# First projections of a two-layer kernel: shift and scale from feature-major weights on VectorE, the next k-tile prepared during this one's products

## Chip, cores and metric

The kernel runs on one core of a Trainium2 chip. The metric is device time in microseconds (us) of one execution; lower is better. All inputs are float32 in HBM and the output is float32.

## What is computed

Two layers run one after the other on 256 tokens of width 1024. The change is in the very first step of the first layer: the shift and scale that come from the condition vector `c`, the normalised and modulated input `h`, and the first columns of `h @ w_in`. Cut to what matters:

```
def rmsnorm(x, g):
    xf = x.astype(jnp.float32)
    xf = xf * lax.rsqrt(jnp.mean(xf * xf, axis=-1, keepdims=True) + EPS)
    return xf.astype(x.dtype) * g
...
    c_act = jax.nn.silu(c)
...
    mod = c_act @ ada_w + ada_b
    sh1, sc1, gt1, sh2, sc2, gt2 = [m[:, None, :] for m in jnp.split(mod, 6, axis=-1)]

    h = rmsnorm(x, mix_pre_g) * (1.0 + sc1) + sh1
    proj = h @ w_in
```

After it follow a state-space branch and a short convolution, a feed-forward block, and a second layer with two kinds of attention and another feed-forward block. None of their arithmetic is touched.

## The kernel before

Everything is kept transposed, features on the 128 partitions and the 256 tokens along a row. The width of 1024 is therefore 8 k-tiles. For each k-tile `t` the first stage makes `h(t)`, a 128x256 tile, and multiplies it with 1568 columns of `w_in` (12 blocks of 128 and one of 32), adding up over `t` in six PSUM banks `xbc` and in a part of the bank `dtps`.

Products in float32 precision are made from two reduced-precision parts: an operand is split into a rounded part `hi` (ScalarE, the CAST rows) and a remainder `lo` (VectorE, the TENSOR_TENSOR rows `lo<-raw,hi`). Each block then takes three products: hi by hi, hi by lo and lo by hi (`mm3`), so a k-tile has 39 products. For `h` the parts are called `hh` and `hl` in the rows. The weights come in halves ("units"), for the first stage of 768 and 800 columns, later of 1024. Six buffers `raw` take what the DMA brings, and five pairs of buffers hold `hi` and `lo`. A unit may thus be cast up to five ahead of the products; a new `lo` waits until TensorE has done with the unit five before it.

Shift and scale for k-tile `t` need 256 columns of `ada_w` (128 of each), all 1024 rows of them: `ada0[t]`, two tiles `ada0a` and `ada0b` of 512 KB each, in the order of the loop also 512 KB to a DMA. The rows of `ada_w` lie on partitions, so the sum over them is a sum over partitions. `mod_acc` lets VectorE multiply six of the eight row blocks by `silu(c)` (one column `cact[:, k]` of 128 values per block) and add them up in `ada0acc` (one TENSOR_SCALAR and five SCALAR_TENSOR_TENSOR instructions of 128x256). `mod_sum` lets TensorE multiply the other two blocks by `cact`, and add `ada0acc` by a product with `ones`: six matmuls of one column, each two rows in the trace because their operands are float32. Then VectorE adds the bias (`m<-ps,pf`), `mod_h` makes `hf` and `hh` on ScalarE, and `mod_lo` makes `hl` on VectorE. These matmuls of k-tile `t + 1` stand in TensorE's order in the middle of k-tile `t`, between `half(0)` and `half(1)`.

Ahead of the loop stand the sums of squares of `x` (`sq`, then products with `ones` into `dtps`), the inverse root (VectorE, then a power on GpSimd), its spreading over the partitions by two products with `ident`, the scaling of `x` by it (the first k-tile on VectorE, the other seven on GpSimd), and 20 products of `ones` with `ones` that only keep TensorE active.

The order of this stage is written out by hand on every engine. DMAs go out in program order on one queue, SyncE's; a load of a `raw` buffer waits there until VectorE has made the `lo` from it, and what stands behind it waits too. After the loop a planner takes over: it keeps a model time of every engine and picks the next piece of work from a list of tasks; a task `caster` casts the units ahead, with the highest priority while fewer than five are ready. So what this stage leaves behind (how many units are ready, where each engine stands) moves the planner's order after it.

Later in the same kernel, other parts of `ada_w` are stored with their features on partitions. There one VectorE instruction multiplies a 128x1024 tile by `crow`, which is `silu(c)` on every partition, and sums along the row (`ada_mul`; CUSTOM_DVE_ANT_0 `raw<-raw,crow` in the trace, with a small instruction behind it that reads the sum out).

Of the kernel before, what the change touches and what calls it, by code (L numbers as in the profile page):

```python
# [31 lines left out]
def _plan():  # L32
# [21 lines left out]
    def b_list(w, k0, nk, cols):  # L54
        return lambda i: (i[w][k0 * 128:(k0 + nk) * 128][:, cols].reshape(nk, 128, len(cols))
                          .transpose(1, 0, 2).reshape(128, -1))

    for t in range(8):
        cols = np.concatenate([np.arange(128) + 128 * t, np.arange(128) + 1024 + 128 * t])
        plan.append((("ada0", t), 2048, b_list("ada_w", 0, 8, cols)))  # L60
        c2 = np.concatenate([np.arange(128) + XBC0 + 128 * f for f in XBC_FT0] + [np.arange(32) + DT0])
        plan.append((("w0", t), 1568, b_list("w_in", t, 1, c2)))
    for g in range(4):
# [175 lines left out]
WARM = 20  # L239
SPLIT0, EARLY = 8, 2  # L240
ROT_SPARE = 6
UPORDER = ("0a 0b 1a 0l 1b 1l", "0a 0b 1a 1b 0l 1l")
LAST_C = "gt1"
# [172 lines left out]
def _body(ctx: ExitStack, tc: tile.TileContext, wst, pf_d, rows_d, cst_d, xT_d, x_d, w2_d, out_d):  # L416
# [18 lines left out]
    def P(name, j=0, n=1, parts=128):  # L435
        return pf[:parts, PF[name][0] + j:PF[name][0] + j + n]
# [203 lines left out]
    def ab(src, j):  # L640
        return src[:, j * T:j * T + T]
# [162 lines left out]
    nc.sync.dma_start(cst[:, 128:], cst_d[:, 128:ROT0])  # L804
    ada0_dma(3)
    cact = const.tile([128, 16], F32, name="cact")
    AC.activation(cact, P("c", 0, 16), AF.Silu)
    xbc = [bank() for _ in range(6)]
    dtps, adps = bank(), bank()
    h = HL("h")  # L810
    acc0, m01 = {}, {}
    PK = (0, 2, 2, 2, 2, 2, 2, 2)

    def ws0(t, k):
        return ada0[t][k // 4].rearrange("p (k c) -> p k c", k=4)[:, k % 4]

    def mod_acc(t, k0, k1):

        if t < 8:
            if k0 == 0:  # L820
                acc0[t] = fresh1("ada0acc")
                VE.tensor_scalar(acc0[t], ws0(t, PK[t]), cact[:, PK[t]:PK[t] + 1], None, op0=OP.mult)
            for k in range(max(k0, PK[t] + 1), k1):
                VE.scalar_tensor_tensor(acc0[t], ws0(t, k), cact[:, k:k + 1], acc0[t], op0=OP.mult, op1=OP.add)

    def mod_sum(t):
        a = acc0.pop(t)
        for j in range(2):
            o = adps[:, 2 * t + j:2 * t + j + 1]
            for k in range(PK[t]):  # L830
                PE.matmul(o, ws0(t, k)[:, 128 * j:128 * j + 128], cact[:, k:k + 1], start=k == 0, stop=False)
            PE.matmul(o, a[:, 128 * j:128 * j + 128], ones[:, 0:1], start=PK[t] == 0, stop=True)
        del ada0[t]
        ada0_dma(t + 4)
        m = m01[t] = sm.tile([128, 2], F32, name="m01")
        VE.tensor_add(m, adps[:, 2 * t:2 * t + 2], P("b01", 2 * t, 2))
        VE.scalar_tensor_tensor(m[:, 1:2], m[:, 1:2], 1.0, P("g1", t), op0=OP.add, op1=OP.mult)
# [11 lines left out]
    sq = ep.tile([128, 2048], F32, name="sq", tag="E")  # L849
    def cast0():  # L850
        O.cur = _Task(None, 0.0)
        if st["cast"] < 2 * len(keys):
            cast_next()
        O.cur = None

    for _ in range(WARM):
        PE.matmul(xbc[0][:, :128], ones, ones, start=True, stop=True)
    for q in range(4):
        AC.activation(sq[:, 512 * q:512 * q + 512], xT[:, 512 * q:512 * q + 512], AF.Square)
        for k in (2 * q, 2 * q + 1):  # L860
            for t in range(2):
                PE.matmul(dtps[:, t:t + 1], sq[:, 256 * k + 128 * t:256 * k + 128 * t + 128], ones[:, 0:1], start=k == 0 and t == 0,
                          stop=k == 7, skip_group_check=True)
    r2 = sm.tile([128, 2], F32, name="r2")
    mod_acc(0, 0, SPLIT0)
    rsqrt(r2, dtps[:, :2], D, 1e-6)
    mod_acc(0, SPLIT0, 8)
    for t in range(2):
        PE.matmul(dtps[:, 128 + 128 * t:256 + 128 * t], r2[:, t:t + 1].to_broadcast([128, 128]), ident, start=True, stop=True)
    if EARLY > 0:  # L870
        cast0()
    mod_sum(0)
    rs = fresh1("rs")
    AC.copy(rs, dtps[:, 128:384])
    VE.tensor_mul(xTv[:, 0], xTv[:, 0], dtps[:, 128:384])
    for t in range(1, 8):
        GP.tensor_mul(xTv[:, t], xTv[:, t], rs)
    if EARLY > 1:
        cast0()
    hf = mod_h(0)  # L880
    if EARLY < 1:
        cast0()
    mod_lo(0, hf)
    if EARLY < 2:
        cast0()
    mod_acc(1, 0, 8)
    cast0()
    cast0()
    for t in range(8):
        w = W(t)  # L890

        def half(hf_):
            for f in range(6 * hf_, 6 * hf_ + 6):
                mm3(ab(xbc[f // 2], f % 2), w, f * 128, 128, h.hi(t), h.lo(t), t == 0 and f % 2 == 0, t == 7,
                    skip_group_check=True)
            if hf_:
                mm3(dtps[:32, :T], w, 1536, 32, h.hi(t), h.lo(t), t == 0, t == 7)
            parts.pop((t, hf_))
            st["half"] += 1
            st["ahead"] -= 1  # L900

        mod_acc(t + 2, 0, 4)
        cast0()
# [8 lines left out]
        cast0()  # L912
        half(1)
    free(adps)

    O.spawn(caster(), lambda: -1 if st["ahead"] < PHASE[phase[0]][1] else 2)
# [1539 lines left out]
```

## Time and profile before

| | |
|---|---|
| median of 3 runs | 1071.05 us (1067.59 to 1071.38) |
| the profiled execution | 1072.64 us |
| its span, first to last instruction | 1070.7 us |
| TensorE busy | 1036.2 us, 97% of the span |
| VectorE busy | 849.8 us, 79% |
| ScalarE busy | 628.4 us, 59% |
| GpSimd busy | 45.7 us, 4% |
| mean granted clock of TensorE | 0.982 |

A busy share is an average over the whole span. TensorE is busy nearly all the time, so the places where it stands still, and those where it does work that another engine could do, are what there is to look for. Idle time of another engine costs nothing as long as TensorE does not wait for it.

### The profile page before, as it was taken

What the parts mean: (1) busy time and instruction counts of PE and PEld (TensorE: products, weight loads), DVE (VectorE), ACT (ScalarE), POOL (GpSimd) and SP (SyncE); (2) the same over time, 40 slices, a digit from 0 to 9 for tenths busy, and PEclk for the clock granted to TensorE, in tenths of its full rate; (3) what the DMA queues carried; (4) which work ended last, traced back from release to release, by engine and by line L of the source; (5) the groups of instructions that cost most, each with busy time, mean ns of one, the idle gap of its engine ahead of it and who ended that gap; (6) DMA issues with size and microseconds to landing.
All of it is one profiled execution on the core that took longest, in us unless ns stands there. A gap on an engine that the chain in (4) does not pass through costs nothing.

```text
span 1070.7 us, 18920 instructions
## 1 busy us (share of the span) xinstructions
PE 1036.2 (97%) x7183; PEld 957.1 (89%) x7183; DVE 849.8 (79%) x1566; ACT 628.4 (59%) x1230; POOL 45.7 (4%) x66
## 2 busy tenths in 40 slices
PE   7999999999999999999999889998999789999998
PEld 7999999899999979999987779877998679999986
DVE  5878978977987768998886888896889687878843
ACT  3457569378654366656554466768675346666531
POOL 2000000000000000000000010221100000000000
PEclk8999999999999999999999989998999989999999
DMA  9855577767868947676686588854256725555551
GB/s 356 310 197 170 176 244 242 238 208 242 284 211 305 328 171 227 223 262 222 225 302 201 188 304 281 291 204 139 77 159 231 281 91 195 180 181 183 188 185 40
DMA packets 66187, 234.03 MB, mean 219 GB/s; under 512 B 7568, under 2 KB 8624, under 8 KB 65584
## 3 DMA queue, kind: packets, MB, share of 16 engines
q1 hardware_dynamic: 66096, 232.82, 64.4%
q8 instruction: 56, 0.92, 0.3%
q14 instruction: 35, 0.29, 0.1%
HBM read 230.67 MB, written 2.13 MB: 217 GB/s over the span
## 4 chain that ended last, share of the span: by engine, by line
PE 52%; DVE 5%; ACT 3%; DMA 2%; issue 1%; POOL 0%; ACTq 0%; DVEq 0%; POOLq 0%
PE ps L410 52%; DVE lo L410 2%; DMA raw<-in_wst_dram 1%; ACT hi L410 1%; DMA adp<-in_wst_dram 1%; ACT S L410 1%; DVE S L410 1%; ACT jk L410 0%; DVE raw L410 0%; DVE jk L410 0%; DVE ropet L410 0%; DVE qo L410 0%; DVE Sm L410 0%; DVE tmp L410 0%; ACT tmp L410 0%
## 5 line engine op out<-in xcount | busy, mean ns | idle before, releaser
L410 DVE TENSOR_TENSOR lo<-raw,hi 128x1024 fp32r<-128x1024 f32 (+3 forms) x326 | 388.2, 1197 | 149.0 <-ACT hi L410 147.9
L410 ACT CAST hi<-raw 128x1024 fp32r<-128x1024 f32 (+3 forms) x326 | 332.9, 1031 | 216.2 <-PE ps L410 170.5
L410 PE MATMUL ps<-hh,hi 128*128 128x256 f32 (+1 forms) x520 | 152.8, 294 | 4.1 <-ACT hh L410 4.1
L410 PE MATMUL ps<-hl,hi 128*128 128x256 f32 (+1 forms) x520 | 148.8, 286 | 0.5 <-DVE hl L410 0.4
L410 PE MATMUL ps<-hh,lo 128*128 128x256 f32 (+1 forms) x520 | 148.6, 286 | 0.0
L410 PEld LDWEIGHTS ps<-hh,hi 128*128 128x128 f32 (+1 forms) x520 | 100.4, 193 | 5.9 <-ACT hh L410 4.5
L410 PE MATMUL ps<-h4h,hi 128*128 128x256 f32 x352 | 100.9, 289 | 2.8 <-ACT h4h L410 2.8
L410 PEld LDWEIGHTS ps<-hl,hi 128*128 128x128 f32 (+1 forms) x520 | 100.4, 193 | 2.3 <-issue 1.2
L410 PE MATMUL ps<-h4h,lo 128*128 128x256 f32 x352 | 100.7, 288 | 0.0
L410 PEld LDWEIGHTS ps<-hh,lo 128*128 128x128 f32 (+1 forms) x520 | 100.4, 193 | 0.1
L410 PE MATMUL ps<-h2h,hi 128*128 128x256 f32 x352 | 98.4, 283 | 0.0
L410 PE MATMUL ps<-h2h,lo 128*128 128x256 f32 x352 | 98.3, 283 | 0.0
L410 PE MATMUL ps<-h2l,hi 128*128 128x256 f32 x352 | 94.7, 283 | 0.0
L410 PE MATMUL ps<-h4l,hi 128*128 128x256 f32 x352 | 94.5, 283 | 0.0
L410 DVE CUSTOM_DVE_ANT_0 raw<-raw,crow 128x1024 f32<-128x1024 f32 x64 | 76.9, 1219 | 0.0
L410 DVE SCALAR_TENSOR_TENSOR fc<-ps,pf,fc 128x254 f32<-128x254 f32 (+1 forms) x176 | 72.4, 474 | 0.0
L410 PEld LDWEIGHTS ps<-h4h,hi 128*128 128x128 f32 x352 | 69.6, 198 | 3.0 <-ACT h4h L410 3.0
L410 PEld LDWEIGHTS ps<-h4h,lo 128*128 128x128 f32 x352 | 69.5, 197 | 0.0
L410 PEld LDWEIGHTS ps<-h2h,hi 128*128 128x128 f32 x352 | 67.6, 192 | 0.8 <-ACT h2h L410 0.8
L410 PEld LDWEIGHTS ps<-h2h,lo 128*128 128x128 f32 x352 | 67.6, 192 | 0.0
L410 PEld LDWEIGHTS ps<-h2l,hi 128*128 128x128 f32 x352 | 65.4, 192 | 0.0
L410 PEld LDWEIGHTS ps<-h4l,hi 128*128 128x128 f32 x352 | 65.4, 192 | 0.0
(394 smaller groups left out, 2363.6 us busy)
## 6 DMA issues: line engine op xcount, KB each, us to landing
raw<-in_wst_dram SPq DMA_DIRECT2D x364, 512.0 KB, 4.9
adp<-in_wst_dram SPq DMA_DIRECT2D x16, 512.0 KB, 7.2
ada0a<-in_wst_dram SPq DMA_DIRECT2D x8, 512.0 KB, 8.0
ada0b<-in_wst_dram SPq DMA_DIRECT2D x8, 512.0 KB, 8.7
E<-scr SPq DMA_DIRECT2D x4, 1024.0 KB, 6.8
raw<-in_wst_dram SPq DMA_DIRECT2D x8, 400.0 KB, 7.5
raw<-in_wst_dram SPq DMA_DIRECT2D x8, 384.0 KB, 7.3
brow<-in_rows_dram SPq DMA_DIRECT2D x4, 512.0 KB, 7.9
```

The costliest lines, as they stand in the source:

```text
L410: return f(*a, **k)
```

## The change

The weights for shift and scale are stored with features on partitions (the transpose is made on the host, like all other arrangement of weights). VectorE makes each sum with one 128x1024 instruction (`mod_dot`), two for a k-tile, and TensorE takes no part in it. `crow` is loaded right behind `x`, and its silu is made at the start. The casts of a k-tile's two units, its two sums and its bias (`start_cast`, `mod_dot`, `mod_end`) are put ahead of the products of the k-tile before it, and the remainders (`end_cast`, `mod_lo`) behind them in the program's text; all eight k-tiles of `x` are scaled on VectorE, one in each step (`scale_x`). Ahead of the loop, two of the four squares go to VectorE, the inverse root comes before the sums for shift and scale, `h(0)` is made in a shorter way, and its first six blocks are taken pass by pass, with the `lo` of `h` last. The products that keep TensorE active are in three groups of 12, 5 and 6. The loop ends with two units cast ahead instead of four.

```diff
-        cols = np.concatenate([np.arange(128) + 128 * t, np.arange(128) + 1024 + 128 * t])
-        plan.append((("ada0", t), 2048, b_list("ada_w", 0, 8, cols)))
+        plan.append((("ada0", t), 2048, lambda i, t=t: np.concatenate([i["ada_w"][:, o + 128 * t:o + 128 * t + 128].T for o in (0, 1024)], 1)))
...
+    crow = wk.tile([128, 1024], F32, name="crow", bufs=1)
+    row_load(crow, "c")
     nc.sync.dma_start(cst[:, :128], cst_d[:, :128])
...
-    AC.activation(cact, P("c", 0, 16), AF.Silu)
...
-    def mod_acc(t, k0, k1):
+    def mod_dot(t, j):

         if t < 8:
...
+            w = ada0[t][j]
+            VE.tensor_tensor_reduce(out=w, in0=w, in1=crow, scale=1.0, scalar=0.0, op0=OP.mult, op1=OP.add,
+                                    accum_out=m01[t][:, j:j + 1])
+            if j == 1:
+                del ada0[t]
+                ada0_dma(t + 4)
+
+    def mod_end(t):
+        if t < 8:
+            m = m01[t]
+            VE.tensor_add(m, m, P("b01", 2 * t, 2))
+            VE.scalar_tensor_tensor(m[:, 1:2], m[:, 1:2], 1.0, P("g1", t), op0=OP.add, op1=OP.mult)
+
+    def scale_x(t):
+        if t < 8:
+            VE.tensor_mul(xTv[:, t], xTv[:, t], rs)
...
+    def start_cast():
...
+        AC.copy(h_[:, :b - a], r)
...
+    def end_cast(l_, r, h_):
+        VE.tensor_sub(l_, r, h_.bitcast(F32))
+        refill()
...
+    warm(WARM[0])
     for q in range(4):
-        AC.activation(sq[:, 512 * q:512 * q + 512], xT[:, 512 * q:512 * q + 512], AF.Square)
...
+        if q % 2:
+            VE.tensor_mul(o, i, i)
+        else:
+            AC.activation(o, i, AF.Square)
+    AC.activation(crow, crow, AF.Silu)
+    AC.activation(cact, P("c", 0, 16), AF.Silu)
...
+    warm(WARM[1])
     r2 = sm.tile([128, 2], F32, name="r2")
-    mod_acc(0, 0, SPLIT0)
     rsqrt(r2, dtps[:, :2], D, 1e-6)
-    mod_acc(0, SPLIT0, 8)
+    mod_dot(0, 0)
+    mod_dot(0, 1)
...
-    mod_sum(0)
-    rs = fresh1("rs")
-    AC.copy(rs, dtps[:, 128:384])
-    VE.tensor_mul(xTv[:, 0], xTv[:, 0], dtps[:, 128:384])
-    for t in range(1, 8):
-        GP.tensor_mul(xTv[:, t], xTv[:, t], rs)
...
+    warm(WARM[2])
+    mod_end(0)
+    m0 = m01.pop(0)
+    y0 = fresh1("hf")
+    VE.scalar_tensor_tensor(y0, xTv[:, 0], m0[:, 1:2], rs_ps, op0=OP.mult, op1=OP.mult)
+    cast0()
+    AC.activation(h.hi(0), y0, AF.Identity, bias=m0[:, 0:1])
+    VE.scalar_tensor_tensor(h.lo(0), y0, m0[:, 0:1], h.hi(0).bitcast(F32), op0=OP.add, op1=OP.subtract)
+    rs = fresh1("rs")
+    AC.copy(rs, rs_ps)
     cast0()
-    cast0()
+    scale_x(1)
...
-        mod_acc(t + 2, 0, 4)
-        cast0()
-        mod_acc(t + 2, 4, 6)
+        if t < 7:
...
+            r = [start_cast() for _ in range(2)]
...
+        mod_dot(t + 1, 0)
+        mod_dot(t + 1, 1)
+        mod_end(t + 1)
         half(0)
+        half(1)
         if t < 7:
-            mod_sum(t + 1)
             hf = mod_h(t + 1)
-        mod_acc(t + 2, 6, 8)
-        if t < 7:
+            end_cast(*r[0])
             mod_lo(t + 1, hf)
-        cast0()
-        half(1)
+            end_cast(*r[1])
+        else:
+            cast0()
+            cast0()
+        scale_x(t + 2)
...
-    crow_load("c")
```

What stands in the engines' orders at three places follows; in such a row the output stands left of the arrow, and `ps_87` to `ps_94` are the PSUM banks.

VectorE, one step of the loop before (`m_434` holds shift and scale of one k-tile):

```order
L410 TENSOR_SCALAR ada0acc<-ada0a,cact 128x256
L410 SCALAR_TENSOR_TENSOR ada0acc<-ada0a,cact,ada0acc 128x256
L410 TENSOR_TENSOR lo<-raw,hi 128x768
L410 SCALAR_TENSOR_TENSOR ada0acc<-ada0b,cact,ada0acc 128x256 x2
L410 TENSOR_TENSOR m_434<-ps_94,pf 128x2
L410 SCALAR_TENSOR_TENSOR m_434<-m_434,pf 128x1
L410 SCALAR_TENSOR_TENSOR ada0acc<-ada0b,cact,ada0acc 128x256 x2
L410 TENSOR_TENSOR hl_223<-hf,hh_222 128x256
L410 TENSOR_TENSOR lo<-raw,hi 128x800
```

VectorE, one step of the loop of the change (the ISA rows are the sum along a row and the reading out of it):

```order
L408 ISA ada0a,m_287<-ada0a,crow 128x1024
L408 ISA m_287 128x1
L408 ISA ada0b,m_287<-ada0b,crow 128x1024
L408 ISA m_287 128x1
L408 TENSOR_TENSOR m_287<-m_287,pf 128x2
L408 SCALAR_TENSOR_TENSOR m_287<-m_287,pf 128x1
L408 TENSOR_TENSOR lo<-raw,hi 128x768
L408 TENSOR_TENSOR hl_204<-hf,hh_203 128x256
L408 TENSOR_TENSOR lo<-raw,hi 128x800
L408 TENSOR_TENSOR xT<-xT,rs 128x256
```

Six multiplications of 128x256 give way to two of 128x1024, the scaling of `x` has come in, and the bias no longer reads the PSUM bank `ps_94`.

TensorE, in the middle of a k-tile before: the end of `half(0)`, the matmuls of `mod_sum`, and the first of `half(1)`:

```order
L410 MATMUL ps_89<-hl_223,hi 128x256
L410 MATMUL ps_89<-hh_222,lo 128x256
L410 MATMUL ps_94<-cact,ada0a 128x1 x2
L410 MATMUL ps_94<-ones,ada0acc 128x1
L410 MATMUL ps_94<-cact,ada0a 128x1 x2
L410 MATMUL ps_94<-ones,ada0acc 128x1
L410 MATMUL ps_90<-hh_222,hi 128x256
```

The same place in the change, in its second k-tile:

```order
L408 MATMUL ps_89<-hh_203,hi 128x256
L408 MATMUL ps_89<-hl_204,hi 128x256
L408 MATMUL ps_89<-hh_203,lo 128x256
L408 MATMUL ps_90<-hh_203,hi 128x256
L408 MATMUL ps_90<-hl_204,hi 128x256
```

The six matmuls (twelve rows of the trace) are gone, and nothing stands in their place.

ScalarE, the head of its order before:

```order
L410 ACT_TABLE_LOAD
L410 ACTIVATE cact<-pf 128x16
L410 ACTIVATE sq<-xT 128x512 x4
L410 CAST hi<-raw 128x768
L410 COPY rs<-ps_93 128x256
```

And in the change:

```order
L408 ACT_TABLE_LOAD
L408 ACTIVATE sq<-xT 128x512 x2
L408 ACT_TABLE_LOAD
L408 ACTIVATE crow<-crow 128x1024
L408 ACTIVATE cact<-pf 128x16
L408 CAST hi<-raw 128x768
L408 ACTIVATE hh_203<-hf,m_178 128x256
```

Two squares are gone to VectorE, a second load of a table stands behind the other two, and a silu of 1024 columns has come in ahead of the first cast. Behind the loop, the orders of all engines differ in places over about the first third of the program, and are the same from there on.

## Rows read from the trace of the kernel before

**Rows 1.** Busy time in four stretches (instructions); last: granted clock, DMA share, GB/s.

```profile
20.00:30.00 10.00, 7.81 (x51) 7.23 (x51) 9.13 (x18) 2.72 (x5) 1.73 (x2) 0.84 1.03 407
70.80:200.00 129.20, 129.20 (x967) 123.18 (x967) 110.12 (x174) 88.23 (x140) 0.00 (x0) 1.00 0.65 215
580.00:590.00 10.00, 7.34 (x40) 5.95 (x38) 7.50 (x14) 7.85 (x19) 1.62 (x3) 1.00 0.41 154
```

**Rows 2.** Timeline of TensorE at the start: start, length, what, idle before and releaser.

```profile
7.72 3.63 PE L410 MATMUL ps<-ones,sq 128*128 128x1 f32 x32
13.80 1.22 PE L410 MATMUL ps<-cst,r 128*128 128x128 f32 x4 [2.45 <-POOL r L410]
...
17.71 0.58 PE L410 MATMUL ps<-hh,hi 128*128 128x256 f32 x1 [2.04 <-ACT hh L410]
...
28.83 0.38 PE L410 MATMUL ps<-hh,hi 128*128 128x256 f32 x1 [2.07 <-ACT hh L410]
...
30.42 0.41 PE L410 MATMUL ps<-hh,hi 128*128 128x256 f32 x1
30.63 0.41 PE L410 MATMUL ps<-hl,hi 128*128 128x256 f32 x1
```

**Rows 3.** Timeline of TensorE: first product of the last k-tile, and of the next stage.

```profile
66.78 0.28 PE L410 MATMUL ps<-hh,hi 128*128 128x256 f32 x1
...
71.45 0.40 PE L410 MATMUL ps<-hi,hh 128*128 128x512 f32 x1
```

**Rows 4.** Timeline of VectorE in one steady step of the loop.

```profile
52.38 0.16 DVE L410 TENSOR_TENSOR m<-ps,pf 128x2 f32<-128x2 f32 x1 [0.21 <-PE ps L410]
52.57 0.16 DVE L410 SCALAR_TENSOR_TENSOR m<-m,pf 128x1 f32<-128x1 f32 x1
...
53.84 0.43 DVE L410 TENSOR_TENSOR hl<-hf,hh 128x256 fp32r<-128x256 f32 x1 [0.20 <-ACT hh L410]
54.61 0.99 DVE L410 TENSOR_TENSOR lo<-raw,hi 128x800 fp32r<-128x800 f32 x1 [0.34 <-ACT hi L410]
...
56.30 0.95 DVE L410 TENSOR_TENSOR lo<-raw,hi 128x768 fp32r<-128x768 f32 x1
...
58.38 0.16 DVE L410 TENSOR_TENSOR m<-ps,pf 128x2 f32<-128x2 f32 x1 [0.21 <-PE ps L410]
```

**Rows 5.** Timeline of ScalarE in the same step.

```profile
52.77 0.61 ACT L410 ACTIVATE hf<-xT,m 128x256 f32<-128x256 f32 x1 [3.06 <-DVE m L410]
53.40 0.41 ACT L410 CAST hh<-hf 128x256 fp32r<-128x256 f32 x1
```

**Rows 6.** Timeline of VectorE: two sums along a row with `crow`, one behind the other.

```profile
206.22 1.22 DVE L410 CUSTOM_DVE_ANT_0 raw<-raw,crow 128x1024 f32<-128x1024 f32 x1
...
207.37 1.22 DVE L410 CUSTOM_DVE_ANT_0 raw<-raw,crow 128x1024 f32<-128x1024 f32 x1
...
208.60 1.23 DVE L410 TENSOR_TENSOR lo<-raw,hi 128x1024 fp32r<-128x1024 f32 x1
```

**Rows 7.** Timelines of ScalarE, VectorE and GpSimd ahead of the loop.

```profile
0.73 1.28 ACT L410 ACT_TABLE_LOAD   x1 [0.73 <-PEq L2448]
...
6.75 1.15 ACT L410 ACTIVATE sq<-xT 128x512 f32<-128x512 f32 x2 [0.20 <-DMA xT<-in_xT_dram]
10.58 0.83 ACT L410 CAST hi<-raw 128x768 fp32r<-128x768 f32 x1 [2.68 <-DMA raw<-in_wst_dram]
...
8.25 0.35 DVE L410 TENSOR_SCALAR ada0acc<-ada0a,cact 128x256 f32<-128x256 f32 x1 [8.25 <-DMA ada0a<-in_wst_dram]
...
12.47 1.28 POOL L410 TENSOR_TENSOR r<-r,nhalf 128x2 f32<-128x2 f32 x1 [11.48 <-DVE r L410]
```

**Rows 8.** Timeline of VectorE behind the stage: convolutions of one bank, and the next `lo`.

```profile
74.88 2.41 DVE L410 SCALAR_TENSOR_TENSOR cv<-ps,pf,cv 128x255 f32<-128x255 f32 x6
77.22 1.20 DVE L410 TENSOR_TENSOR lo<-raw,hi 128x1024 fp32r<-128x1024 f32 x1
78.35 2.41 DVE L410 SCALAR_TENSOR_TENSOR cv<-ps,pf,cv 128x255 f32<-128x255 f32 x6
```

More of the change, by code (lines that the diff above doesn't have):

```diff
@@ L238 @@
 MARGIN = 0.0
-WARM = 20
-SPLIT0, EARLY = 8, 2
+WARM = (12, 5, 6)
 ROT_SPARE = 6
@@ L810, in _body @@
     h = HL("h")
[L811 to L815, printed above, removed]
-    def mod_acc(t, k0, k1):
-        if t < 8:
[L820 to L837, printed above, removed]
+    m01 = {}
+    def mod_dot(t, j):
+        if t < 8:
+            if t not in m01:
+                m01[t] = sm.tile([128, 2], F32, name="m01")
+            w = ada0[t][j]
[12 more added lines that the diff above has]
+            VE.tensor_mul(xTv[:, t], xTv[:, t], rs)
     def mod_h(t):
@@ L849, in _body @@
     sq = ep.tile([128, 2048], F32, name="sq", tag="E")
+    def start_cast():
+        u = st["cast"]
+        a, b = span(u)
+        r = raws.pop(u)[:, :b - a]
+        h_, l_ = hlp.tile([128, 1024], F32R, name="hi"), hlp.tile([128, 1024], F32R, name="lo")
+        AC.copy(h_[:, :b - a], r)
+        cast_at[divmod(u, 2)] = 0.0
+        parts[divmod(u, 2)] = (h_, l_)
+        st["ahead"] += 1
+        st["cast"] += 1
+        return l_[:, :b - a], r, h_[:, :b - a]
+    def end_cast(l_, r, h_):
+        VE.tensor_sub(l_, r, h_.bitcast(F32))
+        refill()
     def cast0():
@@ L854, in cast0, with warm @@
         O.cur = None
-    for _ in range(WARM):
-        PE.matmul(xbc[0][:, :128], ones, ones, start=True, stop=True)
+    def warm(n):
+        for _ in range(n):
+            PE.matmul(adps[:, :128], ones, ones, start=True, stop=True)
+    warm(WARM[0])
     for q in range(4):
-        AC.activation(sq[:, 512 * q:512 * q + 512], xT[:, 512 * q:512 * q + 512], AF.Square)
[L860 to L863, printed above, removed]
+        o, i = sq[:, 512 * q:512 * q + 512], xT[:, 512 * q:512 * q + 512]
+        if q % 2:
+            VE.tensor_mul(o, i, i)
+        else:
+            AC.activation(o, i, AF.Square)
@@ L864, in _body @@
+    AC.activation(crow, crow, AF.Silu)
+    AC.activation(cact, P("c", 0, 16), AF.Silu)
+    for k in range(8):
+        for t in range(2):
+            PE.matmul(dtps[:, t:t + 1], sq[:, 256 * k + 128 * t:256 * k + 128 * t + 128], ones[:, 0:1], start=k == 0 and t == 0,
+                      stop=k == 7, skip_group_check=True)
+    warm(WARM[1])
     r2 = sm.tile([128, 2], F32, name="r2")
-    mod_acc(0, 0, SPLIT0)
     rsqrt(r2, dtps[:, :2], D, 1e-6)
-    mod_acc(0, SPLIT0, 8)
+    mod_dot(0, 0)
@@ L868, in _body @@
+    mod_dot(0, 1)
+    rs_ps = dtps[:, 128:384]
     for t in range(2):
-        PE.matmul(dtps[:, 128 + 128 * t:256 + 128 * t], r2[:, t:t + 1].to_broadcast([128, 128]), ident, start=True, stop=True)
-    if EARLY > 0:
-        cast0()
-    mod_sum(0)
-    rs = fresh1("rs")
-    AC.copy(rs, dtps[:, 128:384])
-    VE.tensor_mul(xTv[:, 0], xTv[:, 0], dtps[:, 128:384])
-    for t in range(1, 8):
-        GP.tensor_mul(xTv[:, t], xTv[:, t], rs)
-    if EARLY > 1:
-        cast0()
-    hf = mod_h(0)
@@ L881, in _body @@
-    if EARLY < 1:
-        cast0()
[L883 to L886, printed above, removed]
+        PE.matmul(rs_ps[:, 128 * t:128 * t + 128], r2[:, t:t + 1].to_broadcast([128, 128]), ident, start=True, stop=True)
+    warm(WARM[2])
[6 more added lines that the diff above has]
+    VE.scalar_tensor_tensor(h.lo(0), y0, m0[:, 0:1], h.hi(0).bitcast(F32), op0=OP.add, op1=OP.subtract)
@@ L892, in half @@
         def half(hf_):
-            for f in range(6 * hf_, 6 * hf_ + 6):
+            if t == 0 and hf_ == 0:
+                for p, (u, x) in enumerate(((0, h.hi(0)), (1, h.hi(0)), (0, h.lo(0)))):
+                    for f in range(6):
+                        PE.matmul(ab(xbc[f // 2], f % 2), w.hi(f * 128, 128, u), x, start=p == 0 and f % 2 == 0,
+                                  stop=False, skip_group_check=True)
+            for f in range(6 * hf_, 6 * hf_ + 6) if t or hf_ else ():
                 mm3(ab(xbc[f // 2], f % 2), w, f * 128, 128, h.hi(t), h.lo(t), t == 0 and f % 2 == 0, t == 7,
@@ L900, in half @@
             st["ahead"] -= 1
-        mod_acc(t + 2, 0, 4)
-        cast0()
-        mod_acc(t + 2, 4, 6)
+        if t < 7:
+            O.cur = _Task(None, 0.0)
+            r = [start_cast() for _ in range(2)]
+            O.cur = None
+        mod_dot(t + 1, 0)
+        mod_dot(t + 1, 1)
+        mod_end(t + 1)
         half(0)
+        half(1)
         if t < 7:
-            mod_sum(t + 1)
             hf = mod_h(t + 1)
-        mod_acc(t + 2, 6, 8)
-        if t < 7:
+            end_cast(*r[0])
             mod_lo(t + 1, hf)
-        cast0()
-        half(1)
+            end_cast(*r[1])
[3 more added lines that the diff above has]
+        scale_x(t + 2)
     free(adps)
@@ L929, in _body @@
     ADA2 = ("sha", "sca", "ga", "shf", "scf", "gf")
-    crow = wk.tile([128, 1024], F32, name="crow", bufs=1)
-    crow_is = []
+    crow_is = ["c", True]
     def crow_load(c):
```

1 line of the change is left out of this document (removed).

## The prediction

> **What bounds the kernel now.** I read first the windows, to see whether TensorE waits, then its timeline at the start, then the other engines in one step of the loop. From 70.8 to 200 us TensorE is busy in every microsecond at the full granted clock [rows 1]; an earlier start of that stretch moves the end by as much, if nothing in it begins to wait. The start is different. The first product of the first k-tile comes at 17.71 us, the second k-tile has to wait 2.07 us for `hh`, and behind that wait the products again come 0.21 us apart [rows 2]. The last k-tile takes 71.45 - 66.78 = 4.67 us for its 39 products, 0.12 us each [rows 3]. Yet a steady step of the loop takes 58.38 - 52.38 = 6.00 us [rows 4]. TensorE does not wait in it: the other 1.33 us are the six matmuls of `mod_sum`, which the last k-tile alone doesn't have. So the stage is bound at first by VectorE and the data, then by TensorE itself, and the small matmuls are a fifth of its step. Behind it nothing waits.
>
> **The loop without the small matmuls.** They leave TensorE 4.67 us of work per k-tile, so VectorE must be costed next. On it, neighbours begin about 0.08 us before the length of the one ahead is over, as the two sums show: two with their reading take 208.60 - 206.22 = 2.38 us though each lasts 1.22 [rows 6]. Then comes the bias, 0.19 from its start to the start of the scale [rows 4]. From there a chain over ScalarE leads to `hl`: `hf` begins at 52.77 and `hh` ends at 53.81 [rows 5], `hl` starts at 53.84, 1.27 us after the scale [rows 4]. The remainder of 768 columns (0.95) fits into that gap and leaves some 0.3 us idle. Then `hl` (0.35 of its 0.43), the remainder of 800 (0.91 of 0.99) and the scaling of `x`, a product of 128x256 with both inputs in SBUF like `hl` (0.35). Together 2.38 + 0.19 + 1.27 + 0.35 + 0.91 + 0.35 = **5.45 us** a step. That is above 4.67: the bound goes from TensorE to VectorE, and of the 1.33 us only 0.55 are kept per step. If the scale's result came so early that nothing idled it would be 5.1 us; I take 5.45, since the change keeps the order scale, `hf`, `hh`, `hl` of these rows. ScalarE has 0.83 + 0.86 for two casts and 1.04 for `hf` and `hh`, under 3 us a step, and is not the bound.
>
> **The head.** The second half of `x` is there at 6.75 us, as before [rows 7], since the load of `crow` stands behind it. The four squares, two on each engine, end at about 7.4. The 16 sums (32 rows) take 3.63 us [rows 2]; of the 20 warming products that end there at 7.72, 12 are left and end before the squares are ready at 6, so the sums are done at 9.7 instead of 11.35. The inverse root is no longer behind eight multiplications on VectorE: 0.2 for the first instruction, then 1.28 on GpSimd [rows 7] to 11.5, then the spreading, at most 1.22 [rows 2], to 12.7. Beside that run the sums for shift and scale. `ada0a` was there at 8.25; `crow` puts 0.5 MB ahead of it, 1.3 us at the 407 GB/s that the DMA moves here [rows 1], so 9.6. `crow` itself lands near 8.1, then a table load of 1.28 [rows 7] behind the squares and a silu of 1024 columns, about 1.1 by the 0.83 of a cast of 768: ready at 9.7. VectorE starts the sums when it has issued the root, at 10.1, has both at 12.4 and the scale at 12.9; the first `hf` 0.43 later, `hh` 0.6 after that (lengths as in [rows 4, 5]). The first weights, cast at 10.58 before, come 1.3 later and are cast by 12.8. So the first product comes at about **14.1** instead of 17.71. If the six last warming products run at 0.21 us a row they end at 15.4 and hold it up; that touches only TensorE's own slack below. VectorE goes on: `hl`, the remainder of 800 (its cast waits behind `hh` and the copy of `rs`), the scaling of the second k-tile; the loop's first step begins at about 16.6.
>
> **The feed.** A k-tile needs 1.05 MB of `ada_w` and 0.80 MB of `w_in`, 4.55 us at 407 GB/s, less than a step. But the queue also carries 0.56 MB of constants early, and now the fifth k-tile's `ada_w` goes ahead of the fourth's weights. Counted from 11.9 us, when the first 768 columns land, those of the fourth k-tile are 7.6 MB further on: 30.5 us. The third step (begun at 16.6 + 2 x 5.45 = 27.5) would have its `hl` begun at 31.3; the cast behind the late half and `hf`, `hh` put it at 32.4. That costs 1.1 us once; afterwards the data lead.
>
> **The sum for the stage.** The last step's `hl` ends at 16.6 + 6 x 5.45 + 1.1 + (2.57 + 1.27 + 0.43) = 54.7; with 39 products of 0.12 behind it the next stage begins at 59.3 instead of 71.45: **12.1 us earlier**. TensorE has 0.78 us of slack in a step, so that a first k-tile at 0.21 us a product (8.2 us) is caught up with by the fourth.
>
> **Behind the stage.** The lead in cast units falls from four to two at the loop's end, and that cover had a use: VectorE then has six times a bank's convolutions and a `lo`, 78.35 - 74.88 = 3.47 us a pair [rows 8], while a unit of 24 products feeds TensorE for 24 x 0.12 = 2.87. Six pairs lose 3.6 us of lead. Counted from the stage's end at 59.3, the third and fourth unit are cast only after the last k-tile lets ScalarE go on, the first convolution starts at 65.3, and the `lo` behind the sixth pair is ready at 65.3 + 6 x 3.47 = 86.1, where TensorE wants it at 59.3 + 9 x 2.87 = 85.1. So TensorE loses about **1.0 us** here; between nothing (if the units come first) and the 3.6 us that the pairs lose. Further on VectorE is busy 110 of 129 us up to 200 us [rows 1], so the backlog drains. The new order of tasks over the first third can make or lose some waits; before there was none to win up to 200 us, so I charge 0.6, bounds 0 and 3.
>
> Removed elsewhere: seven products on GpSimd and a later load and silu of `crow`, which are off TensorE's path; I price them at nothing. Were the cover gone (ScalarE late at that place), it would be the one silu, about 1.1 us.
>
> Sum: -12.1 + 1.0 + 0.6 = **-10.5 us**. The profiled execution took 1072.64 us, span 1070.7; the median of the runs is 1071.05, 0.15% below it. From the median: **1060.5 us**.
>
> **Rivals.** *TensorE keeps the bound.* If VectorE's chain is shorter than I count (5.1 a step, no late data), the stage ends at 56 and the gain is 13 to 15 us: 1056 to 1058; the floor, 14.1 + 8 x 4.67 = 51.5, would be 1051. For it speaks that all row lengths are upper ones; against it the chain over ScalarE, which is measured.
>
> *The lead is lost and not won back.* The planner starts with two units fewer, and if TensorE then waits for `lo` or a bank several times before 200 us, the 3.6 us of the pairs plus the 3 us of other order are lost: gain 4 to 7, 1064 to 1067. For it speaks that VectorE is 85% busy there.
>
> *The clock falls in every step; this would make it slower.* In a VectorE-bound loop TensorE waits in every k-tile, 0.78 us by my count and longer in the second and fourth. Behind the wait of 2.07 us the products came 0.21 us apart [rows 2], the 1.2 GHz level of the granted clock instead of 2.4. At that pace a k-tile takes 8.2 us, and eight of them 65.6: the stage would end near 80, 8 us later than before, 1079. It decides from about four k-tiles at the lower level on (10.5 over 8.2 - 5.45). Against it: from 580 to 590 us TensorE is idle for 2.66 of 10 us and the clock stays at 1.00 [rows 1], and at the lower level the waits vanish, since 8.2 is more than a step, and TensorE at work without a break got the clock back (0.84 over 20 to 30 us, with that wait in it [rows 1]). This is the pattern against which the Trainium skill speaks ("TensorE: Matmul & The Clock Gate", section "HAM oscillation — how this bites in real kernels"): a loop whose matmul group is shorter than the wait for its next slice falls back to the half clock in each k-tile and begins each one cold. By that rule the time would be the 1079 above; the trace of before shows such a fall at the second k-tile only, behind a wait near half a k-tile's work, and my waits are a sixth of it.
>
> *Nothing comes of it.* The feed or a later chain sets the time anyway. The last weights land near 46 us by the same count, nine before they are used, so this is weak.
>
> **Chances.** Forecast (VectorE paces the stage, 1057 to 1064) 0.62; TensorE keeps the bound 0.13; lead lost 0.17; clock 0.04; nothing 0.04. The range from 1055 to 1067 takes in the first three but for their tails. A change under 0.5% (5.4 us) can hardly be told from none here: the three runs of before lie 0.35% apart. Faster than that: 0.62 + 0.13 and two thirds of the third, 0.87; within: 0.08; slower: 0.05.
>
> **What would show it.** In the profile after: first product near 14 us; a step near 5.45 us on VectorE, read between two rows of the bias; TensorE waiting under 1 us in each step for `hh` or `hl`; the first 512-column product near 59 us; a few short waits for `lo` up to 100 us. I am wrong if a step takes 6 us or more (slower sums, or a cast that waits), if the clock shows 0.5 over several k-tiles, or if waits behind the stage add up to more than 5 us.

## The result, and the profile after

The change takes **1063.02 us** (median of 7 runs, 1062.15 to 1065.97) against 1071.33 us for the kernel before (7 runs, 1067.59 to 1072.5): a ratio of **0.993, 95% interval 0.9914 to 0.9946**. That is 8.3 us less where 10.5 were forecast. The profiled execution took 1063.29 us, its span is 1061.5 us and its mean granted clock 0.988.

The first view is the windows, as in [rows 1]: length, busy time of PE, PEld, DVE, ACT and POOL with instructions, granted clock, DMA share, GB/s.

```profile
9.00:15.00 6.00, 6.00 (x29) 6.00 (x30) 3.54 (x9) 1.95 (x4) 1.62 (x1) 0.50 1.02 416
20.00:30.00 10.00, 9.08 (x69) 8.07 (x68) 9.42 (x19) 3.72 (x6) 0.00 (x0) 1.00 1.03 408
30.00:40.00 10.00, 7.97 (x60) 6.97 (x59) 7.96 (x17) 5.31 (x8) 0.00 (x0) 1.00 1.03 408
60.80:200.00 139.20, 139.14 (x1020) 131.37 (x1019) 118.85 (x182) 91.13 (x144) 0.00 (x0) 1.00 0.66 221
```

VectorE is now busy 9.42 of the 10 us from 20 to 30. From 30 to 40 it falls to 7.96 and TensorE to 7.97, with the DMA moving as much as before (408 GB/s): there the data are late. In the head, from 9 to 15 us, TensorE never stops and yet has only half the clock.

TensorE's timeline answers to [rows 2, 3]; the last two rows are the first product of the next stage, and the first with `h2h`, which ends the stretch in which the two kernels' orders differ.

```profile
6.23 4.79 PE L408 MATMUL ps<-ones,sq 128*128 128x1 f32 x32 [0.27 <-ACT sq L408]
...
13.15 1.11 PE L408 MATMUL ps<-cst,r 128*128 128x128 f32 x4
14.05 2.20 PE L408 MATMUL ps<-ones 128*128 128x128 f32 x12
16.00 0.96 PE L408 MATMUL ps<-hh,hi 128*128 128x256 f32 x6
...
33.77 0.38 PE L408 MATMUL ps<-hh,hi 128*128 128x256 f32 x1 [1.56 <-ACT hh L408]
...
60.81 0.40 PE L408 MATMUL ps<-hi,hh 128*128 128x512 f32 x1
...
392.01 0.39 PE L408 MATMUL ps<-h2h,hi 128*128 128x256 f32 x1
```

The same last row in the kernel before:

```profile
398.48 0.39 PE L410 MATMUL ps<-h2h,hi 128*128 128x256 f32 x1
```

The stage ends at 60.81 instead of 71.45, 10.64 us earlier. At `h2h` only 398.48 - 392.01 = 6.47 us are left: between the two rows the kernel before took 327.0 us and the change takes 331.2, so 4.2 us are given back.

VectorE's timeline has one step of the loop, to be read against [rows 4], and the late `hl` of the fourth k-tile:

```profile
17.61 1.22 DVE L408 CUSTOM_DVE_ANT_0 ada0a<-ada0a,crow 128x1024 f32<-128x1024 f32 x1
...
20.21 0.16 DVE L408 SCALAR_TENSOR_TENSOR m<-m,pf 128x1 f32<-128x1 f32 x1
20.29 0.96 DVE L408 TENSOR_TENSOR lo<-raw,hi 128x768 fp32r<-128x768 f32 x1
21.48 0.42 DVE L408 TENSOR_TENSOR hl<-hf,hh 128x256 fp32r<-128x256 f32 x1 [0.23 <-ACT hh L408]
21.82 0.98 DVE L408 TENSOR_TENSOR lo<-raw,hi 128x800 fp32r<-128x800 f32 x1
22.72 0.42 DVE L408 TENSOR_TENSOR xT<-xT,rs 128x256 f32<-128x256 f32 x1
23.06 1.22 DVE L408 CUSTOM_DVE_ANT_0 ada0a<-ada0a,crow 128x1024 f32<-128x1024 f32 x1
...
33.75 0.42 DVE L408 TENSOR_TENSOR hl<-hf,hh 128x256 fp32r<-128x256 f32 x1 [1.00 <-ACT hh L408]
```

The step is 23.06 - 17.61 = 5.45 us, with 1.27 from the scale to `hl`: the 0.96 of a remainder and 0.23 idle. ScalarE shows what made the fourth k-tile late:

```profile
12.32 0.83 ACT L408 CAST hi<-raw 128x768 fp32r<-128x768 f32 x1 [2.39 <-DMA raw<-in_wst_dram]
...
30.92 0.83 ACT L408 CAST hi<-raw 128x768 fp32r<-128x768 f32 x1 [4.03 <-DMA raw<-in_wst_dram]
31.92 0.86 ACT L408 CAST hi<-raw 128x800 fp32r<-128x800 f32 x1 [0.17 <-DMA raw<-in_wst_dram]
32.68 0.60 ACT L408 ACTIVATE hf<-xT,m 128x256 f32<-128x256 f32 x1
```

Both casts stand ahead of `hf` in its order, and each waits for its own load; `hf` could have started at about 31.3 by its scale, whose instruction of 0.16 us starts at 31.11.

Last, TensorE's waits from 60 to 400 us (total, times, longest). The kernel before has only the one for `btok`.

```profile
PE ps L408 <- DVE yscl L408: 1.6, 1, 1.6
PE ps L408 <- DVE yTl L408: 1.0, 1, 1.0
PE ps L408 <- DVE btok L408: 0.6, 1, 0.6
```

`yscl` and `yTl` are remainders of the state-space branch. So the open question is what gave the 4.2 us back: the lead of two cast units, VectorE's backlog, or the planner's order.

### The profile page after: what moved, and what is told of

Same layout as the page of the kernel before. It is cut to its first block, busy times and chain, and to the rows that moved or that the text cites. A ratio compares the mean times of both kernels' runs of the same rounds, so it can differ in the third digit from the quotient of the medians.

```text
span 1061.5 us, 18723 instructions
## 1 busy us (share of the span) xinstructions
PE 1027.2 (97%) x7101; PEld 945.2 (89%) x7101; DVE 847.2 (80%) x1557; ACT 625.8 (59%) x1228; POOL 37.1 (3%) x59
## 4 chain that ended last, share of the span: by engine, by line
PE 66%; DVE 6%; ACT 4%; issue 2%; DMA 1%; POOL 0%; SPq 0%; ACTq 0%; DVEq 0%; POOLq 0%
PE ps L408 66%; DVE lo L408 2%; DMA adp<-in_wst_dram 1%; ACT hi L408 1%; ACT S L408 1%; DVE raw L408 1%; DVE S L408 1%; ACT jk L408 0%; DVE jk L408 0%; DVE ropet L408 0%; ACT junk L408 0%; DVE qo L408 0%; DVE Sm L408 0%; POOL ssk L408 0%; DVE tmp L408 0%
## 5 line engine op out<-in xcount | busy, mean ns | idle before, releaser
L408 PE MATMUL ps<-hh,hi 128*128 128x256 f32 (+1 forms) x520 | 150.4, 291 | 3.1 <-ACT hh L408 3.1
```

Source lines behind the costliest of these rows:

```text
L408: return f(*a, **k)
```

## The experiments

The three columns of stretches are read from the profiled execution of each kernel: "stage" is the start of the first 512-column product, the next column the time from there to the first product with `h2h`, the third what is left of the span. The last column is the median of the timed runs, and of how many.

| kernel | stage | stage to `h2h` | `h2h` to the end | time, us |
|---|---|---|---|---|
| before | 71.45 | 327.0 | 672.2 | 1071.33 (7) |
| the change | 60.81 | 331.2 | 669.5 | 1063.02 (7) |
| pk0 | 74.85 | 347.1 | 668.6 | 1092.34 (1) |
| gapfill | 59.89 | 331.3 | 667.3 | 1060.31 (1) |
| lateconst | 59.43 | 331.2 | 671.5 | 1063.86 (1) |
| dotfirst | 60.61 | 331.2 | 668.6 | 1062.13 (1) |
| same_order | 60.53 | 327.0 | 671.9 | 1059.09 (4) |
| lead4 | 60.60 | 327.0 | 667.5 | 1056.94 (1) |
| lead3 | 60.72 | 328.2 | 670.6 | 1061.24 (1) |
| charge2 | 60.68 | 337.0 | 667.5 | 1066.98 (1) |
| the change again | 60.73 | 331.3 | 667.6 | 1062.15 (10) |
| all_edits | 57.37 | 327.0 | 667.8 | 1054.91 (4) |
| lead4_edits | 58.53 | 327.0 | 668.5 | 1057.92 (4) |

The stretch up to `h2h` repeats within 0.1 us where the order is the same. The one behind it lies between 667 and 672, with no relation to the edits that can be seen, and 1.9 us apart for the change and its repeat; so a single total can't tell 2 us, and the stretches can. What it does go with is TensorE's granted clock: in the four kernels whose last stretch is over 670 us (before, lateconst, same_order, lead3) the clock stood at 0.50 for 22.3 to 25.7 us of it, in the other nine for 11.4 to 19.1.

### The stage: what paces it

**pk0** takes four of the six matmuls off TensorE and gives their work to VectorE as it stands: the kernel before, with all eight row blocks multiplied on VectorE.

```diff
-    PK = (0, 2, 2, 2, 2, 2, 2, 2)
+    PK = (0, 0, 0, 0, 0, 0, 0, 0)
```

> One part alone, on the kernel before: all eight row blocks of a k-tile's shift and scale on VectorE, so that TensorE keeps two one-column matmuls instead of six, with the weights still row-major and the order of before. TensorE's step falls from 6.00 to about 5.1 us; VectorE's has two more multiplications of 0.40 and comes to 5.6 to 5.9. If VectorE paces once TensorE is relieved, the step is 5.6 to 5.9 us and the first 512-column product comes 1 to 3 us earlier than 71.45: relief of TensorE alone is worth little, the cheap sums are what the change needs. If TensorE's matmuls are all that matters, the step is 5.1 and the product comes 5 us or more earlier.

It took 1092.34 us beside 1069.05 for the kernel before. The expected step of 5.6 to 5.9 us was missed, and the stage ends 3.4 us later instead of 1 to 3 us earlier. TensorE's timeline, first product of three k-tiles, then its waits over the whole span:

```profile
44.44 0.39 PE L410 MATMUL ps<-hh,hi 128*128 128x256 f32 x1 [1.02 <-ACT hh L410]
51.17 0.39 PE L410 MATMUL ps<-hh,hi 128*128 128x256 f32 x1 [1.02 <-ACT hh L410]
57.90 0.38 PE L410 MATMUL ps<-hh,hi 128*128 128x256 f32 x1 [1.02 <-ACT hh L410]
```

```profile
PE ps L410 <- ACT hh L410: 8.3, 7, 2.0
PE ps L410 <- DVE xs L410: 7.7, 1, 7.7
PE ps L410 <- DVE lo L410: 4.2, 3, 2.9
...
PE ps L410 <- DVE cv L410: 2.0, 1, 2.0
```

A step is 6.73 us. With two more multiplications VectorE paces the loop at more than TensorE's old 6.00: taken off TensorE in this way, the matmuls make the stage slower, and the change gains because its two long sums shorten VectorE's step at the same time. And behind the stage, where no work was changed, a new order lost 20 us: 13.9 are the waits for `xs`, `lo` and `cv`, and in the same stretch the granted clock stood at 0.50 for 13.7 us, which before has nowhere in it.

**gapfill** puts the scaling of `x` into VectorE's idle time ahead of `hl`.

```diff
             end_cast(*r[0])
+            scale_x(t + 2)
             mod_lo(t + 1, hf)
...
-        scale_x(t + 2)
```

> One edit to the change: in each step the scaling of x stands between the remainder of 768 columns and hl, in the gap in which VectorE waits for hh. If VectorE's chain paces the stage, a step falls from 5.45 to about 5.12 us, and the first 512-column product, at 60.8 us in the change, comes at about 59.2: the four steps behind the late data of the fourth k-tile keep the gain, the first ones give theirs back there. If TensorE or the transfers pace it, the step stays near 5.4 and the product at 60.8.

VectorE's timeline, `hl` of the third to the seventh k-tile:

```profile
25.54 0.42 DVE L408 TENSOR_TENSOR hl<-hf,hh 128x256 fp32r<-128x256 f32 x1
...
33.74 0.42 DVE L408 TENSOR_TENSOR hl<-hf,hh 128x256 fp32r<-128x256 f32 x1 [0.65 <-ACT hh L408]
...
39.33 0.42 DVE L408 TENSOR_TENSOR hl<-hf,hh 128x256 fp32r<-128x256 f32 x1
...
44.49 0.42 DVE L408 TENSOR_TENSOR hl<-hf,hh 128x256 fp32r<-128x256 f32 x1
...
49.65 0.42 DVE L408 TENSOR_TENSOR hl<-hf,hh 128x256 fp32r<-128x256 f32 x1
```

The step falls to 5.16 us (49.65 - 44.49), so the gap was the 0.3 us the forecast named. The loop starts at 16.52, yet the fourth `hl` comes at 33.74, as in the change: what is won ahead of the late data is lost there. The stage ends at 59.89, not 59.2, since of the steps behind the late data the first is no shorter than in the change (39.33 - 33.74 = 5.59).

**lateconst** takes the constants out of the early queue.

```diff
-    nc.sync.dma_start(pf[:, PF_HEAD:], pf_d[:, PF_HEAD:])
-    nc.sync.dma_start(cst[:, 128:], cst_d[:, 128:ROT0])
...
+        if t == 4:
+            nc.sync.dma_start(pf[:, PF_HEAD:], pf_d[:, PF_HEAD:])
+            nc.sync.dma_start(cst[:, 128:], cst_d[:, 128:ROT0])
```

> One edit to the change: the two loads of constants, 0.56 MB, that stand ahead of the fourth k-tile's ada_w are issued inside the loop, behind the weights of the last k-tile. If the fourth k-tile's weights are late in the change (the cast of its units waits for the transfer until 30.92 and 31.92 us, and hl starts at 33.75 instead of 32.4), they come 1.4 us earlier here, hl starts at its usual distance from the scale, and the first 512-column product comes at 59.5 instead of 60.8. If that step is late for another reason, nothing moves.

The cast of the fourth k-tile starts at 29.57 instead of 30.92, its `hl` at 32.38 instead of 33.75, and the stage ends at 59.43, 1.38 us earlier: the delay of the data passes to the end one for one. But `hl` isn't at its usual distance from the scale, as was expected: the third step still takes 6.13 us (27.83 to 33.96), so the data are late here too, by 0.7. (The total is no better in this run, by its last stretch of 671.5.)

**dotfirst** puts the first two sums ahead of the inverse root, x last.

```diff
+    mod_dot(0, 0)
+    mod_dot(0, 1)
     rsqrt(r2, dtps[:, :2], D, 1e-6)
-    mod_dot(0, 0)
-    mod_dot(0, 1)
```

> One edit to the change: the two sums for the first k-tile go ahead of the inverse root again, as the multiplications did before, so x is no longer first on VectorE. The root's first instruction goes from 11.05 to about 12.2 us and the first product from 16.0 to about 17. If the stage is held by late data at the fourth k-tile, this delay of 1.1 us is swallowed there (hl of that k-tile at 33.8 under both) and the first 512-column product stays at 60.8 to 61.0: putting x first then bought nothing. If VectorE's chain from the first sum to the last is unbroken, the product comes 1.1 us later, at 61.9.

The root starts at 12.26 instead of 11.05, though not by the edit alone: in this run the sums of squares took 5.75 us, to 12.1. The first product comes at 17.51 and the loop starts at 18.65, 1.04 later than in the change. The fourth `hl` stands at 33.56 and the stage ends at 60.61, 0.2 earlier. So "x first" bought nothing here, as long as the fourth k-tile's data come at 31 us.

### Behind the stage: what gave 4.2 us back

**same_order** casts four units at the loop's end, and starts the planner from the model times and charges of the kernel before, so that every engine's order behind the stage is the one of before.

```diff
-            cast0()
-            cast0()
+            for _ in range(4):
+                cast0()
+    O.t.update(pe=51367.0, dve=43382.0, act=38160.0, pool=6840.0, sp=43382.0, dma=46099.0)
...
-    crow_is = ["c", True]
+    crow_is = ["c", False]
+    O.dma(512, O.t["dve"])
...
-            AC.activation(crow, crow, AF.Silu)
+            if crow_is[0] == "c":
+                O.charge("act", (0.0 if AC.tab == "s" else 1300.0) + 1024 / 1.2 + 94.0)
+                AC.tab = "s"
+            else:
+                AC.activation(crow, crow, AF.Silu)
```

> The stage of the change, but the loop ends with four units cast ahead, and the planner is handed the model times that it had in the kernel before at this point, so that every engine's order behind the stage is that of before (the silu of crow left out). In the profile of the change TensorE waits 1.6 us for yscl near 225 us and 1.0 us for yTl near 310 us, waits that before did not have. If they come from the planner's new order, they are gone here and the span falls from 1061.5 to about 1059. If they come from VectorE, which has really less lead behind the shorter stage, they stay or others of 2 to 4 us take their place, above all for lo between 65 and 100 us, since the planner now believes VectorE 8 us further on than it is. The first 512-column product comes at 60.8 us under both.

1059.09 us against 1068.88 for the kernel before on the same chip: a ratio of 0.9908, 0.9884 to 0.9932. TensorE's timeline and its waits from 60 to 400 us:

```profile
60.53 0.40 PE L408 MATMUL ps<-hi,hh 128*128 128x512 f32 x1
...
387.55 0.39 PE L408 MATMUL ps<-h2h,hi 128*128 128x256 f32 x1
```

```profile
PE ps L408 <- DVE btok L408: 0.6, 1, 0.6
```

387.55 - 60.53 = 327.0, and both new waits are gone. All that the stage wins arrives at `h2h`. A VectorE that can't follow a TensorE 11 us ahead of it would have lost here too, so that rival falls for a lead of four units; VectorE's deliveries came earlier with the stage. The rows of `yscl` (first and last start) show by how much, in the kernel before, in same_order and in the change:

```profile
L410 PE MATMUL ps<-yscl,hi x64: 281/283/283, 234.7 to 260.2; 128*128 128x256 f32 x64
L410 DVE TENSOR_TENSOR yscl<-sco,ysch x4: 673/685/687, 129.7 to 226.7; 128x512 fp32r<-128x512 f32 x4
```

```profile
L408 PE MATMUL ps<-yscl,hi x64: 281/283/283, 223.7 to 249.3; 128*128 128x256 f32 x64
L408 DVE TENSOR_TENSOR yscl<-sco,ysch x4: 671/686/689, 118.9 to 215.7; 128x512 fp32r<-128x512 f32 x4
```

```profile
L408 PE MATMUL ps<-yscl,hi x64: 279/283/389, 225.1 to 252.1; 128*128 128x256 f32 x64
L408 DVE TENSOR_TENSOR yscl<-sco,ysch x4: 671/684/685, 119.1 to 228.4; 128x512 fp32r<-128x512 f32 x4
```

With the old order the last part is begun 8.0 us ahead of the first product; with the change's, 3.3 us behind it.

**lead4** changes only the lead, and lets the planner choose its own order.

```diff
-            cast0()
-            cast0()
+            for _ in range(4):
+                cast0()
```

> One edit to the change: the last step casts four units ahead instead of two; the planner keeps its own model times, and so makes an order of its own behind the loop (neither that of before nor that of the change). From the first 512-column product to the first product with h2h took 327.0 us in before and with its order, 331.2 us in the change. If the lead of two units is what costs the 4 us, this stretch takes about 327 here too. If it is the order alone, any value from 327 to 332 can come, with waits for other tiles than yscl and yTl. Setting the model times without the lead needs no run: the order built that way is the change's own, row for row.

327.0 again, by another order than same_order's (`yscl` is 3.7 us ahead of its product). **lead3** does the same with three casts:

```diff
-            cast0()
-            cast0()
+            for _ in range(3):
+                cast0()
```

> One edit to the change: three units cast ahead in the last step, with an order of its own behind. If what the lead takes from VectorE's later work is what costs, this lies between: about 329 us from the first 512-column product to h2h, with 1 to 2 us of waits. If the order alone decides, it can be 327 or over 331. The product itself comes at 60.6 to 60.8 as in the change.

It gave 328.2, with one wait of 0.5 us for `xs`. So far the lead seems to tell. **charge2** keeps the lead of two and moves the order alone, by the charges for the silu and the load of `crow` that same_order also makes (the second hunk and the third of its diff, so neither the lead nor `O.t.update`):

```diff
-    crow_is = ["c", True]
+    crow_is = ["c", False]
+    O.dma(512, O.t["dve"])
```

> The change with its lead of two units, and one thing told to the planner alone: the later silu and load of crow are still charged in its model as before, though they aren't made. No instruction of the stage differs, and the order behind it is the change's up to about 150 us and another one from there. From the first 512-column product to the first with h2h the change took 331.2 us, both orders with a lead of four 327.0. If the lead of two costs the 4 us, this takes 330 to 332 with waits for the same two kinds of tile; if that was this one order's bad luck, about 327.

Both numbers were missed: 337.0 us. The waits for `yscl` and `yTl` are gone, and two for `lo` have come:

```profile
PE ps L408 <- DVE lo L408: 3.5, 2, 2.7
PE ps L408 <- DVE btok L408: 0.6, 1, 0.6
PE ps L408 <- ACT hi L408: 0.3, 1, 0.3
```

At one lead, the order alone is worth 6 us. Not all of the 10 us lost are waits: behind the longer wait for `lo` and behind the other two the granted clock falls to 0.50, for 3.4 us from 183.4 and for 6.8 us from 282.4, where in the change it is 1.00 throughout from 60.8 to 392.

**after_again** is the change itself, run beside pk0, lead4 and all_edits on a chip other than that of same_order.

> The change itself once more, beside the next kernel on the same chip: 0.7 to 0.9% under before, its first 512-column product between 60 and 61 us, and 331 us from there to the first product with h2h.

1062.15 against 1069.05, a ratio of 0.9938 (0.9921 to 0.9956), just under the 0.7% expected, and again 331.3 with the same two waits: the loss belongs to this kernel, its lead and order together, and is no accident of one run.

### All together

**all_edits** is same_order, gapfill and lateconst in one, and sends the weights of the fourth k-tile ahead of the fifth's `ada_w`:

```diff
             if j == 1:
                 del ada0[t]
-                ada0_dma(t + 4)
+                if t:
+                    ada0_dma(t + 4)
...
     cast0()
+    ada0_dma(4)
     scale_x(1)
```

> The change with four edits: the order of before behind the loop, the scaling of x in VectorE's gap, the constants behind the loop's weights, and the fourth k-tile's weights ahead of the fifth's ada_w. If VectorE's chain is then the only thing that paces the stage, its first step begins near 16.7 us, all steps take 5.15, the first 512-column product comes at 56.6 to 57.5, and 327 us follow to h2h: 14 to 15 us less than before, 1.3 to 1.4%. If the late data were only the first of several limits, the product stays above 58; if VectorE has now too little time to work ahead, waits for lo of over 1 us in all show between 60 and 100 us.

**1054.91 us against 1069.05, a ratio of 0.9865 (0.9839 to 0.9891).** VectorE's timeline, the first sum of the third to the fifth step and the `hl` behind two of them:

```profile
27.07 1.22 DVE L408 CUSTOM_DVE_ANT_0 ada0a<-ada0a,crow 128x1024 f32<-128x1024 f32 x1
...
31.00 0.42 DVE L408 TENSOR_TENSOR hl<-hf,hh 128x256 fp32r<-128x256 f32 x1
32.23 1.22 DVE L408 CUSTOM_DVE_ANT_0 ada0a<-ada0a,crow 128x1024 f32<-128x1024 f32 x1
...
36.80 0.42 DVE L408 TENSOR_TENSOR hl<-hf,hh 128x256 fp32r<-128x256 f32 x1
38.04 1.22 DVE L408 CUSTOM_DVE_ANT_0 ada0a<-ada0a,crow 128x1024 f32<-128x1024 f32 x1
```

The third step is 5.16 us: the fourth k-tile is late no more. The fifth now is, by 0.65 (the fourth step is 5.81). The stage ends at 57.37 and nothing is given back behind it.

**lead4_edits** is the same without the planner's charges and times, with lead4's own order.

> The version without anything told to the planner: the change with a lead of four units, the scaling of x in VectorE's gap, the constants behind the loop's weights, and the fourth k-tile's weights ahead of the fifth's ada_w. By the runs so far the first 512-column product comes at 57.4 us as with all four edits and 327.0 us follow, the order being that of lead4, row for row: 1.3 to 1.4% under before. If the stretch behind the stage is sensitive to 3 us more of VectorE's lag, waits for lo appear and it takes 328 or more.

1057.92 against 1070.11, a ratio of 0.989 (0.9869 to 0.9911). Behind the stage it took the expected 327.0, but the stage ended at 58.53, not 57.4: its sums of squares took 5.26 us, and the root began at 11.66 where all_edits has 10.31. With the late data gone, 1.35 us in the head are 1.16 at the stage's end.

## Why the prediction was right, and which terms were not

The sign and the range were right, and the mechanism for the stage was the one forecast. By its steps:

**The step.** 5.45 us forecast, 5.45 measured, by the very chain that was summed; gapfill took the named 0.3 us of idle out of it. The bound went from TensorE to VectorE.

**The head.** First product forecast at 14.1, measured 16.00 (14.86 in the repeat). The step that failed is "the sums are done at 9.7 instead of 11.35". They took 4.79 us where [rows 2] have 3.63, because the granted clock fell to 0.50 in the middle of them, at 8.67 (an estimate: the 2.35 us from there to their end hold 1.18 us of work at full clock, and 4.79 - 1.18 = 3.61); the power on GpSimd also took 1.62, not 1.28. The last warming products held the first product up, as was allowed for. At the stage's end this cost nothing: with loops that start at 16.97 (the repeat), 17.61 and 18.65 (dotfirst) the fourth `hl` stands at 33.66, 33.75 and 33.56.

**The feed.** Here the missing 1.5 us of the stage were lost. The late data came where forecast, 18.6 us behind the first weights (12.32 and 30.92), but these were 0.4 later than taken. And "the cast behind the late half and `hf`, `hh` put it at 32.4" counted one cast; there are two, the second behind a load of its own. `hl` came at 33.75, 1.35 late, and the stage at 60.81 instead of 59.3. lateconst shows that such a delay passes to the end, and that the constants were only a part of what made the data late.

**Behind the stage.** Two terms were mis-sized. The 1.0 for waits on `lo` was nothing: TensorE has no such wait from 60 to 400 us. The 0.6 for the planner's new order, with 3 as its upper bound, was 4.2. Of these, 2.6 are the waits for `yscl` and `yTl`. Most of the other 1.6 isn't waiting: for the same products TensorE is busy 1.3 us longer in that stretch, at a granted clock of 1.00, as the windows of the kernel before and of the change show (columns as above):

```profile
71.40:398.50 327.10, 326.46 (x2407) 306.92 (x2405) 269.36 (x397) 204.40 (x330) 7.63 (x8) 1.00 0.70 236
60.80:392.00 331.20, 327.75 (x2406) 306.98 (x2404) 271.49 (x399) 203.65 (x331) 4.98 (x8) 1.00 0.69 235
```

Part of that lies where one of the large products follows directly on a product with `xw`: it then takes 0.40 us more until the next one (0.52 instead of 0.12 at 200.00 us), and the change's order has eight such places where before's has five. The bound was taken from the lack of waits in the kernel before. A wait that isn't there says nothing on the margin: the last part of `yscl` was begun only 8 us ahead of its first product, 155 us behind the stage, and pk0 and charge2 show that an order can cost 20 and 10 us. Whether the lead of two units or the model times behind it count for more stays open, since each lead brings an order of its own. Four kernels of the new stage with a lead of four, in two orders, lost nothing; two orders at a lead of two lost 4.2 and 10; but pk0 has the lead of four and lost 20.

**The sum.** -10.64 + 4.2 = -6.5 us at `h2h`, where the forecast has -10.5. The span of the profiled run ends up 9.2 shorter, the medians differ by 8.3 and in the repeat by 6.9. The 2.7 us between -6.5 and -9.2 lie in the last stretch, which no edit reaches and which is 1.9 us shorter in the repeat of the same kernel. For the same instructions TensorE is busy there for 646.4 us before and 643.6 in the change, with the granted clock at 0.50 for 24.0 and 18.6 us; half of that difference, an estimate of what it costs, is 2.7. So that part of the gain is taken as luck: with the 6.5 alone the time would be 1064.8, still in the range, but above the 1064 at which the forecast's own case ends.

**The rivals.** *TensorE keeps the bound*: not in the change; all_edits comes near its 56 with 57.37. *The lead is lost*: the gain at `h2h`, 6.5, lies in its 4 to 7, but the loss did not come through `lo`, except in charge2. *The clock falls in every step*: in the profiled run the granted clock was 1.00 throughout from 20 to 60 us. In same_order, gapfill, lead3, charge2 and the repeat it fell to 0.50 once, near 33 us, behind a wait of 2.1 to 2.9 us for the late `hh`. It came back within 3.4 to 6.8 us and stayed; the stage ended between 59.89 and 60.73 all the same, since TensorE had time to spare. That a wait comes before the fall agrees with the Trainium skill ("TensorE: Matmul & The Clock Gate", section "HAM oscillation — how this bites in real kernels"); that every k-tile then begins cold is not what these traces show.

## What to carry to other kernels

When work moves from the bounding engine to another one, cost the receiving engine's whole step, chain included; the sum was exact here, and moving a part of the work (pk0) made it slower. For a late load, count every cast and every load that stands ahead of the consumer in its engine's order. Where a planner or scheduler takes its start from the changed part, write down how early the other engines deliver in the stretch behind it, and try the old order with the new stage: here that was worth 4.2 us in the trace, half of the measured gain (with the lead of four that this order begins from).

## What was not expected of the hardware

- The granted clock fell while TensorE was busy. From 9 to 15 us of the change it shows 6.00 of 6.00 us busy at 0.50, in the sums of one column and the products behind them. In all eleven profiled runs with the new head it fell to 0.50 at some point between 7.7 and 10.6 us, and the sums took 3.72 to 5.75 us; in the kernel before, the same sums ran at 1.00 from 7.8 to 11.3, behind 40 rows of warming products from 0.99 us on, where the change has 24 and a wait of 0.27 us. That these make the difference was not tried.
- The same power of two columns on GpSimd (whose spans the profile gives roughly) took 0.70 us in dotfirst, where VectorE had little to do beside it, 1.28 in the kernel before, beside a remainder of 768 columns, and 1.62 in the change, beside the long sums.
- A half clock cost nothing in this loop, which VectorE paces: same_order, lead3, charge2 and the repeat, each with a fall near 33 us, end the stage at 60.53 to 60.73, and the change, lead4 and dotfirst, without one, at 60.60 to 60.81.
